# ReLU and row sum of a 64 MB tensor: another assignment of rows to partitions in the first 8 MB

## The chip, the cores and the metric

The kernel runs on one core of one Trainium2 chip. The metric is device time in microseconds, the median of several runs; less is better. Nothing else runs on the chip meanwhile.

## The reference

```python
def setup_inputs():
    batch, seq, dim = 32, 512, 1024
    return {"x": np.random.randn(batch, seq, dim).astype(np.float32)}

def reference(x):
    relu_x = np.maximum(x, 0)
    return np.sum(relu_x, axis=-1).astype(np.float32)
```

Negative values are set to zero and each row of 1024 floats is summed. The input has 32 x 512 = 16384 rows of 4 KB, 64 MB (67.11 million bytes) in all; the output is 16384 floats, 64 KB. Every input byte is read once.

## The kernel before

**Layout.** The rows, flattened to 16384 x 1024, are dealt to the 128 partitions of SBUF, 128 rows to each. This is done in two parts. The first `N1 = 128 * 16` rows, 8 MB, are viewed as `xf`: partition p holds rows 16p to 16p+15, one stretch of 64 KB in memory, and the stretches of neighbouring partitions are neighbours in memory. The other 14336 rows, 56 MB, are viewed as `xv`: partition p holds 112 rows one after the other, 448 KB, and a load takes 16 of the 112. So a load of 16 rows per partition always takes 128 contiguous runs of 64 KB; in the first load the runs lie 64 KB apart from one partition to the next, in the others 448 KB. The views `of` and `ov` of the output match `xf` and `xv`; the helpers `rows` and `sums` choose between them.

**Buffers and loads.** There are three buffers `io0` to `io2`, each 128 partitions x 16 rows x 1024 floats (8 MB). Seven loads of 8 MB (`NB = 7`) go round these three. Load j from j = 3 on waits until VectorE has finished with load j-3. The last 8 MB are loaded in smaller parts: 8 rows, 4 rows, and then a few pieces of the last 4 rows (`TAIL`, `START_PIECE`, `END_PIECE`, `PIECES`), so that little work is left when the last byte has landed.

**Who issues.** All loads and stores are issued by SyncE, through one queue (`load`, line 99; `store`, lines 109 and 110). There is no scheduler: the program is written out by hand, with one semaphore for each load, one that counts ScalarE's instructions and one that counts VectorE's. `open_without_barrier` moves the first load to the very start of the program, ahead of the branch into its body (`EARLY = 1`).

**Compute.** For the first five loads and most of the sixth, ScalarE (ACT) clamps the tile in place with a Relu activation (`clamp`, line 117), in one instruction or in two halves, and VectorE (DVE) sums each row with a reduction (`total`, line 125). The last rows are done row by row, with an instruction that clamps and sums at once, on ScalarE (`act_row`, line 132) or on VectorE (`dve_row`, line 140). The results collect in `res`, 128 x 128 floats.

**Stores.** Three at the end: the 16 columns of `res` that belong to the first load, 110 columns of the others, and the last 2.

Of the kernel before, what the change touches and what calls it, by code (L numbers as in the profile page):

```python
# [7 lines left out]
P = 128  # L8

ROWS = 16  # L10
NBUF = 3
# [8 lines left out]
TAIL = [8, 4]  # L20
START_PIECE, END_PIECE = 280, 260
PIECES = [240, 244]

EARLY = 1


def kernel(tc: tile.TileContext, x: bass.AP, out: bass.AP):
    nc = tc.nc
    sems = Semaphores(tc)

    tc.close()
    tc.compile()
    nc.cur_bb = nc.bb_map[tc.start_bb_name]
    body = nc.cur_bb.bb.instructions
    ends = list(body)
    body.clear()
    n_stores = relu_sum(nc, sems, x, out)
    body.extend(ends)


    nc.cur_bb = nc.bb_map[tc.start_bb_name + "_end"]
    nc.cur_bb.bb.instructions.clear()
    nums = sorted(s.num for s in (*sems.loads, sems.act, sems.dve))
    cleared = range(nums[0], nums[-1] + 1)
    assert len(cleared) == len(nums)
    nc.sync.sem_clear(cleared)
    nc.sync.wait_ge(sems.stored, 16 * n_stores).then_inc(sems.stored, -16 * n_stores)
    open_without_barrier(tc, EARLY)


class Semaphores:
    def __init__(self, tc: tile.TileContext):
        n = len(TWO) + len(TAIL) + 2 + len(PIECES)
        self.loads = [tc.alloc_semaphore(f"load{i}") for i in range(n)]
        self.act = tc.alloc_semaphore("act")
        self.dve = tc.alloc_semaphore("dve")
        self.stored = tc.alloc_semaphore("stored")


def relu_sum(nc, sems: Semaphores, x: bass.AP, out: bass.AP):  # L60
    x_flat = x.flatten_outer_dims()
# [3 lines left out]
    assert N == P * NT == P * ROWS * (NB + 1)  # L65
    assert sum(TAIL) == ROWS - 4 and START_PIECE + END_PIECE + sum(PIECES) == D

    bufs = [nc.alloc_sbuf_tensor(f"io{i}", [P, ROWS, D], F32) for i in range(NBUF)]
    res = nc.alloc_sbuf_tensor("res", [P, NT], F32)

    extra = len(PIECES) + 1
    parts = [
        nc.alloc_sbuf_tensor(f"piece{i}", [P, w + extra * (i + 1 == len(PIECES))], F32)
        for i, w in enumerate(PIECES)
    ]


    N1 = P * ROWS
    xf = x_flat[:N1].rearrange("(p m) d -> p m d", p=P)
    xv = x_flat[N1:].rearrange("(p m) d -> p m d", p=P)  # L80
    o_flat = out.rearrange("b s -> (b s)")
    of = o_flat[:N1].rearrange("(p m) -> p m", p=P)
    ov = o_flat[N1:].rearrange("(p m) -> p m", p=P)

    def rows(m, n):
        if m < ROWS:
            return xf[:, m : m + n, :]
        return xv[:, m - ROWS : m - ROWS + n, :]

    def sums(m, n):  # L90
        if m < ROWS:
            return of[:, m : m + n], res[:, m : m + n]
        return ov[:, m - ROWS : m - ROWS + n], res[:, m : m + n]

    n_load = n_act = n_dve = n_store = 0
# [1 line left out]
    def load(dst, src, after=None):  # L97
        nonlocal n_load
        dma = nc.sync.dma_start(out=dst, in_=src)  # L99
        if after:  # L100
            dma.wait_op(sems.dve, after[1], "sem-ge")
        dma.then_inc(sems.loads[n_load], 16)
        n_load += 1
        return sems.loads[n_load - 1]

    def store(m, n, act, dve):
        nonlocal n_store
        dst, src = sums(m, n)
        nc.sync.wait_ge(sems.act, act)
        nc.sync.dma_start(out=dst, in_=src).wait_op(sems.dve, dve, "sem-ge").then_inc(  # L110
            sems.stored, 16
        )
        n_store += 1

    def clamp(ap, loaded):
        nonlocal n_act
        i = nc.scalar.activation(out=ap, in_=ap, func=RELU)  # L117
        if loaded is not None:
            i.wait_op(loaded, 16, "sem-ge")
        i.then_inc(sems.act, 1)  # L120
        n_act += 1

    def total(ap, m, n):
        nonlocal n_dve
        nc.vector.tensor_reduce(  # L125
            out=res[:, m : m + n], in_=ap, axis=mybir.AxisListType.X, op=ADD
        ).wait_op(sems.act, n_act, "sem-ge").then_inc(sems.dve, 1)
        n_dve += 1

    def act_row(ap, accum_out, loaded):  # L130
        nonlocal n_act
        i = nc.scalar.activation(out=ap, in_=ap, func=RELU, accum_out=accum_out)  # L132
        if loaded is not None:
            i.wait_op(loaded, 16, "sem-ge")
        i.then_inc(sems.act, 1)
        n_act += 1

    def dve_row(ap, accum_out, loaded):
        nonlocal n_dve
        i = nc.vector.tensor_scalar(  # L140
            out=ap,
            in0=ap,
            scalar1=0.0,
            scalar2=None,
            op0=MAX,
            op1=ADD,
            accum_out=accum_out,
        )
        if loaded is not None:
            i.wait_op(loaded, 16, "sem-ge")  # L150
        i.then_inc(sems.dve, 1)
        n_dve += 1

    freed = []
    m = 0
    for j in range(NB):
        buf = bufs[j % NBUF]
        loaded = load(buf[:, :, :], rows(m, ROWS), j >= NBUF and freed[j - NBUF])
        c = 0
        act_waits = dve_waits = loaded  # L160
        for n in TWO[j]:
            clamp(buf[:, c : c + n, :], act_waits)
            total(buf[:, c : c + n, :], m + c, n)
            act_waits = None
            c += n
        for _ in range(ACT[j]):
            act_row(buf[:, c, :], res[:, m + c : m + c + 1], act_waits)
            act_waits = None
            c += 1
        for _ in range(DVE[j]):  # L170
            dve_row(buf[:, c, :], res[:, m + c : m + c + 1], dve_waits)
            dve_waits = None
            c += 1
        assert c == ROWS
        freed.append((n_act, n_dve))
        m += ROWS


    buf = bufs[NB % NBUF]
    c = 0  # L180
    for n in TAIL:
        loaded = load(
            buf[:, c : c + n, :], rows(m, n), None if c else freed[NB - NBUF]
        )
        for i in range(n):
            if i % 2 == 0 or (n == 8 and i == 7):
                act_row(buf[:, c, :], res[:, m : m + 1], loaded if i == 0 else None)
            else:
                dve_row(buf[:, c, :], res[:, m : m + 1], loaded if i == 1 else None)
            c += 1  # L190
            m += 1

    flat = buf[:, :, :].rearrange("p c d -> p (c d)")
    src = rows(m, 4).rearrange("p c d -> p (c d)")
    at = c * D
    split = 2 * D
    b = split + START_PIECE
    end = split + D - END_PIECE
    last, w = parts[-1], PIECES[-1]
    others = [last[:, w + i : w + i + 1] for i in range(extra)]  # L200
    loaded = load(flat[:, at : at + b], src[:, :b])
# [5 lines left out]
    loaded = load(flat[:, at + end : at + 4 * D], src[:, end:])  # L207
# [77 lines left out]
```

## Time and profile before

| what | value |
|---|---|
| median of 3 runs | 161.07 us (161.0 to 161.1) |
| the profiled execution, its own time | 160.96 us |
| its span | 159.6 us |
| VectorE busy | 117.6 us, 74% of the span |
| ScalarE busy | 104.2 us, 65% |
| DMA packets, share of 16 engines' span | 98.0% |
| HBM read | 67.11 MB, 421 GB/s over the span |
| ScalarE starts on loads 0, 1, 2 at | 21.87, 41.19, 60.55 us |

The span runs from the first instruction that the profile records to the last; the execution's own time lies 1.4 us above it. "Busy" counts an engine's own instructions, without those that issue transfers. The DMA figures are for the 16 DMA engines of the core, which carry all loads and stores. A DMA packet here is one contiguous run, 64 KB in the 8 MB loads. In a table by stretches of time a packet and its bytes are counted where the packet starts, so a short stretch can show more than the engines can move, and the next one less.

### The profile page before, as it was taken

Reading aid. Unit: us, or ns where it says so; the run is one execution under the profiler, and the core shown is the slowest. Engines: PE = TensorE matmul, PEld = TensorE weight load, DVE = VectorE, ACT = ScalarE, POOL = GpSimd, SP = SyncE. Lnnn points to the kernel's source line nnn. Section 1 sums busy time; section 2 is a strip of 40 time slices with the busy share of each in tenths; the row PEclk is TensorE's granted clock in tenths of the full one; section 3 lists DMA queues with packets and bytes.
Section 4 is the critical chain, followed back from the end, with each engine's and each line's share of the span. In section 5 each row is a group of like instructions: output and inputs, shape, how many; then the busy total and the mean of one; then the engine's idle time right before and its main releaser. Section 6 shows DMA issues by size and latency. Waiting matters only on the chain.

```text
span 159.6 us, 120 instructions
## 1 busy us (share of the span) xinstructions
DVE 117.6 (74%) x43; ACT 104.2 (65%) x50; POOL 0.2 (0%) x4
## 2 busy tenths in 40 slices
DVE  0000000009999499994999999999999999999986
ACT  3000059990699708996099951999329993499995
POOL 0000000000000000000000000000000000000000
DMA  7996996996997999979979969969969969798993
GB/s 279 509 526 263 526 526 263 526 509 279 526 476 312 526 394 394 526 345 443 526 328 460 526 263 526 526 263 526 509 279 526 493 296 526 337 452 382 418 412 119
DMA packets 2304, 67.18 MB, mean 421 GB/s; under 512 B 640, under 2 KB 896, under 8 KB 1024
## 3 DMA queue, kind: packets, MB, share of 16 engines
q1 hardware_dynamic: 2304, 67.18, 98.0%
HBM read 67.11 MB, written 0.07 MB: 421 GB/s over the span
## 4 chain that ended last, share of the span: by engine, by line
DMA 43%; DVE 34%; ACT 17%; another core or an unknown queue 3%; SPq 1%; issue 0%
DMA io<-in_x_dram 43%; DVE res L125 32%; ACT io L117 17%; DVE io L140 1%; SPq L99 1%; DVE piece L224 0%; DVE piece L140 0%
## 5 line engine op out<-in xcount | busy, mean ns | idle before, releaser
L125 DVE TENSOR_REDUCE res<-io 128x8 f32<-128x8192 f32 (+2 forms) x9 | 101.1, 11287 | 40.0 <-ACT io L117 40.0
L117 ACT ACTIVATE io<-io 128x8192 f32<-128x8192 f32 (+2 forms) x9 | 81.7, 9110 | 47.7 <-DMA io<-in_x_dram 47.7
L132 ACT ACTIVATE io<-io 128x1024 f32<-128x1024 f32 x20 | 20.9, 1045 | 6.0 <-DMA io<-in_x_dram 6.0
L140 DVE TENSOR_SCALAR_CACHE_REDUCE io<-io 128x1024 f32<-128x1024 f32 (+2 forms) x15 | 15.8, 1110 | 0.5 <-DMA io<-in_x_dram 0.4
L132 ACT ACTIVATION_READ_ACCUMULATOR io<-io 128x1 f32 x20 | 3.8, 188 | 0.0
L117 ACT ACT_TABLE_LOAD x1 | 1.3, 1283 | 0.1
L140 DVE DVE_READ_ACCUMULATOR io<-io 128x1 f32 x15 | 1.2, 82 | 0.0
L224 DVE TENSOR_SCALAR_CACHE_REDUCE piece<-piece 128x247 f32<-128x247 f32 x1 | 0.4, 410 | 0.0
L140 DVE TENSOR_SCALAR_CACHE_REDUCE piece<-piece 128x240 f32<-128x240 f32 x1 | 0.4, 397 | 0.0
L269 POOL MEMSET const-bfloat16-1.0<- 128x1 bf16 x1 | 0.1, 101 | 0.0
L269 POOL MEMSET const-uint8-127<- 128x1 uint8 x1 | 0.1, 101 | 0.0
L269 POOL MEMSET const-float32-0.0<- 128x1 f32 x1 | 0.1, 98 | 0.2 <-issue 0.2
L269 POOL MEMSET const-float32-1.0<- 128x1 f32 x1 | 0.1, 98 | 0.0
L224 DVE DVE_READ_ACCUMULATOR piece<-piece 128x1 f32 x1 | 0.1, 83 | 0.0
L140 DVE DVE_READ_ACCUMULATOR piece<-piece 128x1 f32 x1 | 0.1, 82 | 0.0
## 6 DMA issues: line engine op xcount, KB each, us to landing
io<-in_x_dram SPq DMA_DIRECT2D x1, 4096.0 KB, 21.6
io<-in_x_dram SPq DMA_DIRECT2D x1, 2048.0 KB, 26.1
io<-in_x_dram SPq DMA_DIRECT2D x1, 1164.0 KB, 28.4
io<-in_x_dram SPq DMA_DIRECT2D x1, 642.0 KB, 29.5
piece<-in_x_dram SPq DMA_DIRECT2D x1, 122.0 KB, 29.2
piece<-in_x_dram SPq DMA_DIRECT2D x1, 120.0 KB, 29.4
io<-in_x_dram SPq DMA_DIRECT2D x7, 26.9
out_dram<-res SPq DMA_DIRECT2D x1, 55.0 KB, 1.6
```

The source lines that it names most:

```text
L99: dma = nc.sync.dma_start(out=dst, in_=src)
L117: i = nc.scalar.activation(out=ap, in_=ap, func=RELU)
L125: nc.vector.tensor_reduce(out=res[:, m : m + n], in_=ap, axis=mybir.AxisListType.X, op=ADD).wait_op(sems.act, n_act, "sem-ge").then_inc(se ...
L132: i = nc.scalar.activation(out=ap, in_=ap, func=RELU, accum_out=accum_out)
L140: i = nc.vector.tensor_scalar(out=ap, in0=ap, scalar1=0.0, scalar2=None, op0=MAX, op1=ADD, accum_out=accum_out,)
L224: nc.vector.tensor_scalar(out=last[:, :], in0=last[:, :], scalar1=0.0, scalar2=None, op0=MAX, op1=ADD, accum_out=res[:, NT - 2 : NT - 1],) ...
L269: nc = _bacc.Bacc("TRN2", target_bir_lowering=False, num_devices=1)
```

## The change

The first 8 MB are cut into 128 stretches of 16 rows, 64 KB each, as before, but they go to other partitions. With `GROUP = 8`, stretch 16j+i (i from 0 to 15, j from 0 to 7) is put into partition 8i+j; before, stretch p was put into partition p. The source of the first load becomes a pattern of three dimensions, 16 (i, 64 KB apart) x 8 (j, 1 MB apart) x 16384 floats, and its destination is the whole buffer as 128 x 16384 floats. The store of the first 16 columns of sums goes through the matching view of the output, so that each sum lands where the reference has it. All other loads and stores, all compute instructions and all waits stay as they are.

```diff
+GROUP = 8
...
     N1 = P * ROWS
-    xf = x_flat[:N1].rearrange("(p m) d -> p m d", p=P)
+    xf = x_flat[:N1].rearrange("(j i m) d -> i j (m d)", j=GROUP, m=ROWS)
     xv = x_flat[N1:].rearrange("(p m) d -> p m d", p=P)
     o_flat = out.rearrange("b s -> (b s)")
-    of = o_flat[:N1].rearrange("(p m) -> p m", p=P)
+    of = o_flat[:N1].rearrange("(j i m) -> i j m", j=GROUP, m=ROWS)
     ov = o_flat[N1:].rearrange("(p m) -> p m", p=P)
 
     def rows(m, n):
-        if m < ROWS:
-            return xf[:, m : m + n, :]
         return xv[:, m - ROWS : m - ROWS + n, :]
 
     def sums(m, n):
         if m < ROWS:
-            return of[:, m : m + n], res[:, m : m + n]
+            return of, res[:, :ROWS]
         return ov[:, m - ROWS : m - ROWS + n], res[:, m : m + n]
...
     for j in range(NB):
         buf = bufs[j % NBUF]
-        loaded = load(buf[:, :, :], rows(m, ROWS), j >= NBUF and freed[j - NBUF])
+        if j == 0:
+            loaded = load(buf[:, :, :].rearrange("p m d -> p (m d)"), xf)
+        else:
+            loaded = load(buf[:, :, :], rows(m, ROWS), j >= NBUF and freed[j - NBUF])
```

## The prediction

> **What bounds the kernel now.** I read the page first, then the busy time by stage, then the chain of waits, then the first microseconds. The page's head and its queue part:
>
> ```profile
> span 159.6 us, 120 instructions
> DVE 117.6 (74%) x43; ACT 104.2 (65%) x50; POOL 0.2 (0%) x4
> ...
> q1 hardware_dynamic: 2304, 67.18, 98.0%
> HBM read 67.11 MB, written 0.07 MB: 421 GB/s over the span
> ```
>
> The reader is to see that no compute engine is near full, while the 16 DMA engines carry packets for 98.0% of the span. Next the busy time in stretches that I cut where the first three loads land (columns: DVE, ACT, POOL, PE clock, DMA share, GB/s):
>
> ```profile
> 0.00:21.85 21.85, 0.00 (x0) 1.28 (x1) 0.20 (x4) 1.00 1.02 432
> 21.85:41.20 19.35, 5.44 (x1) 13.87 (x2) 0.00 (x0) 1.00 1.00 434
> 41.20:60.53 19.33, 17.23 (x2) 13.85 (x1) 0.00 (x0) 1.00 1.00 434
> ```
>
> An 8 MB load takes 19.33 to 19.35 us at 434 GB/s, that is 27.1 GB/s for each of 16 engines, and the DMA share is 1.00. The waits say the same from the consumer's side:
>
> ```profile
> ACT io L117 <- DMA io<-in_x_dram: 47.7, 6, 20.5
> DVE res L125 <- ACT io L117: 40.0, 3, 35.8
> ```
>
> ACT waits for data, DVE for ACT; nothing waits for a free engine. So a microsecond added to or taken from the transfers of the first load moves every later load, and the end, by the same. One slack could absorb it: load 3 needs the buffer of load 0. It was issued at 53.00 us (the timeline, line L99), when loads 1 and 2 still had work until 60.53. But DVE frees that buffer a fixed 13.86 + 17.22 us after load 0 lands, and loads 1 and 2 move with load 0, so the slack of 7.5 us moves along and absorbs nothing.
>
> Last, the first round of packets:
>
> ```profile
> 0.00:1.00 1.00, 0.00 (x0) 0.88 (x1) 0.20 (x4) 1.00 0.00 0
> 1.00:1.40 0.40, 0.00 (x0) 0.40 (x1) 0.00 (x0) 1.00 6.25 2130
> 1.40:1.90 0.50, 0.00 (x0) 0.00 (x1) 0.00 (x0) 1.00 1.02 393
> 1.90:3.90 2.00, 0.00 (x0) 0.00 (x0) 0.00 (x0) 1.00 0.00 0
> 3.90:6.30 2.40, 0.00 (x0) 0.00 (x0) 0.00 (x0) 1.00 1.01 437
> ```
>
> A packet is booked where it starts. 2130 GB/s x 0.40 us is 0.85 MB, so 13 of the 16 first packets of 64 KB start between 1.0 and 1.4 us, the other three by 1.9. Their mean length is (6.25 x 0.40 + 1.02 x 0.50) = 3.01 us, against 19.34 / 8 = 2.42 us for a later one. The first round thus costs 0.59 us more than a later round. That is all that a better place to begin can give back.
>
> [...]
>
> **The change part by part.**
>
> *Compute, later loads, the other stores: nothing.* ACT and DVE see the same 128x16384 tile; their rows are the same in number and shape. The 8 KB store of the first sums goes to 16x8x16 places instead of 128x16, still 64 B each. It took 28.8 us to land behind the last loads; SP has only the two later stores behind it, and the next waits for data until about 155 us. Without that cover it would cost one SP issue, 0.34 us.
>
> *The first load's issue.* The source becomes 16 x 8 x 16384, a pattern with one more dimension. SP's issues at L99 took 327 to 457 ns; the first, at 383 ns, stands ahead of everything. A longer pattern was not seen: at best no change, at worst one more issue, 0.4 us. I take +0.2.
>
> *Where the engines begin in memory.* The 0.59 us of the first round could vanish wholly or not at all (or double). I take -0.3.
>
> *Where the engines write.* This is the large term. [...] each of the 8 packets takes 2 x 2.42 us: 8 x 2.42 = 19.34 us more. [...] with starts mostly within 0.4 us I take L = 0.2, so -0.4. [...]
>
> *Sum:* 19.34 - 0.4 + 0.2 - 0.3 = +18.8 us. The profiled execution has a span of 159.6 and a time of 160.96, 1.4 us around the span; it becomes 179.8. It stands 0.1 us under the median of 161.07, so 179.9 on the median, which I round to 180.0. What is late next is everything: load 0 lands near 40.7 instead of 21.87 us, and loads 1 to 6 keep their spacing.
>
> **Rivals.**
>
> [...] Then only the start counts: 161.07 - 0.59 + 0.2 = 160.7, at best 160.5. [...]
>
> *The pairs fall out of step.* [...] +9.7, about 170.8. The fixed length of packets in the trace (1.00 share in each stage) gives no hint of an order between engines. Partial favour lies between this and the main case, a later drift a little under it: 166 to 176.
>
> *The change doesn't do what it says.* [...] the time is that of before give or take the issue: 161.0 to 161.4.
>
> **How the numbers follow.** Fair sharing 0.65 (177 to 185), out of step 0.17 (166 to 176), [...] nothing changed 0.03, a bare loss at the issue 0.03 (161.4 to 163). From no change a measurement of this kernel can tell about 0.2%, 0.3 us. Slower: 0.65 + 0.17 + 0.03 = 0.85; faster 0.12; same 0.03. The range takes the first two cases, 166 to 185; it leaves out 0.18.
>
> **What would show each step.** In the profile after, the stretch from 0 to the landing of load 0 should run at about 218 GB/s with a DMA share near 1, because packets last 4.8 us instead of 2.42; the first ACT row should start at 40 to 41 us; later loads should land 19.3 us apart as now. Packets of 2.42 us in two groups, with ACT starting near 31.5, would be the out-of-step case. [...] if the mean first packet falls from 3.01 towards 2.42, the near start works. A load 0 far beyond 43 us would mean that reading 64 KB apart costs something by itself, which I do not price.

## The result, and the profile after

The changed kernel takes 182.38 us (median of 4 runs, 182.26 to 182.46) against 161.06 us for the kernel before: a ratio of 1.1324, 95% interval 1.1304 to 1.1343. It is 21.3 us slower, all of it in the first load. The head and the queue part of its page:

```profile
span 181.0 us, 120 instructions
DVE 117.6 (65%) x43; ACT 104.2 (58%) x50; POOL 0.2 (0%) x4
...
q1 hardware_dynamic: 2304, 67.18, 98.0%
...
HBM read 67.11 MB, written 0.07 MB: 371 GB/s over the span
```

The compute engines are busy for the same microseconds as before. The DMA engines move the same bytes in the same number of packets and are still "busy" for 98.0% of the span, yet the rate fell from 421 to 371 GB/s. A busy DMA engine is thus not a DMA engine at full speed: a packet of the first load lasts about 5.1 us instead of 2.42, as the lines below show, and all of it counts as busy. What makes it last is the question of the experiments. The busy time by stage, cut where loads 0, 1 and 2 land (columns: DVE, ACT, POOL, PE clock, DMA share, GB/s):

```profile
0.00:43.20 43.20, 0.00 (x0) 1.28 (x1) 0.20 (x4) 1.00 1.00 218
43.20:62.50 19.30, 5.37 (x1) 13.86 (x1) 0.00 (x0) 1.00 1.00 435
62.50:81.85 19.35, 17.30 (x2) 13.86 (x1) 0.00 (x0) 1.00 1.00 434
```

The DMA share is 1.00 in all three, the rate is half in the first alone. The 218 GB/s of the first line flatter it, as packets are booked where they start: 218 GB/s x 43.20 us is 9.4 MB, so the first packets of load 1 are in it. Loads 1 and 2 follow at 19.3 us as before. The start of that first load, closer:

```profile
1.00:1.40 0.40, 0.00 (x0) 0.40 (x1) 0.00 (x0) 1.00 0.00 0
1.40:2.30 0.90, 0.00 (x0) 0.00 (x0) 0.00 (x0) 1.00 5.24 1165
2.30:5.80 3.50, 0.00 (x0) 0.00 (x0) 0.00 (x0) 1.00 0.00 0
5.80:41.40 35.60, 0.00 (x0) 0.00 (x0) 0.00 (x0) 1.00 1.00 206
```

No packet starts before 1.4 us, where 13 of 16 had. The 16 first packets (1165 GB/s x 0.90 us is 1.05 MB) last 5.24 x 0.90 = 4.72 us on average instead of 3.01; the DMA share, like the bytes, is booked where a packet starts. The other seven rounds fill 35.6 us, 5.09 us each instead of 2.42. The waits and the timeline agree:

```profile
ACT io L118 <- DMA io<-in_x_dram: 69.1, 6, 41.8
...
43.24 13.86 ACT L118 ACTIVATE io<-io 128x16384 f32<-128x16384 f32 x1 [41.84 <-DMA io<-in_x_dram]
...
74.38 0.33 SPq L100 DMA_DIRECT2D io<-in_x_dram  x1
```

ACT starts on load 0 at 43.24 us instead of 21.87, 21.37 us later; load 3 is issued at 74.38 instead of 53.00 us, later by the same; the span ends 21.4 us later. Nothing downstream absorbed any of it.

### The profile page after: what moved, and what is told of

Its sections match the earlier page's. It is cut to its first block, busy times and chain, and to the rows that moved or that the text cites. A ratio compares the mean times of both kernels' runs of the same rounds, so it can differ in the third digit from the quotient of the medians.

```text
span 181.0 us, 120 instructions
## 1 busy us (share of the span) xinstructions
DVE 117.6 (65%) x43; ACT 104.2 (58%) x50; POOL 0.2 (0%) x4
## 4 chain that ended last, share of the span: by engine, by line
DMA 40%; DVE 30%; ACT 23%; another core or an unknown queue 6%; SPq 0%; issue 0%
DMA io<-in_x_dram 40%; DVE res L126 29%; ACT io L118 23%; DVE io L141 1%; SPq L100 0%; DVE piece L228 0%; DVE piece L141 0%
```

## The experiments

Three theories could explain a halved first load: P, engines that write into certain partitions at the same time hold each other up; S, the order in which the engines read memory; F, the three-dimensional pattern itself. The prediction takes it that P doubles the length of every packet, and its 19.34 us rest on that. This was my assumption: nothing in the trace before shows it, and no trace names the engine that writes a partition. They show rates, lengths of packets and the share of engines at work, and it is by these that P is tested. Each kernel below is the kernel before with an altered first load, except the second.

**e1, two plain loads of 64 partitions.**

```diff
-        loaded = load(buf[:, :, :], rows(m, ROWS), j >= NBUF and freed[j - NBUF])
+        if j == 0:
+            w = P // PARTS                 # PARTS = 2
+            for q in range(PARTS):
+                dma = nc.sync.dma_start(
+                    out=buf[q * w : q * w + w, :, :],
+                    in_=xf[q * w : q * w + w, :, :],
+                )
+                dma.then_inc(sems.loads[0], 16)
...
```

> The kernel before, with its first 8 MB loaded as two plain loads of 64 partitions each, partition p still holding stretch p. Theory P [...]: [...] Load 0 lands near 43 us, its stretch runs at 205 to 210 GB/s, the time is 181.5 to 182.5 us. Theory S (the order in which the engines read memory): order as before, about 161 us. Theory F (the three-dimensional pattern is what is slow): plain pattern, about 161 us.

Measured: 182.35 us, one run; ACT starts on load 0 at 43.31 us. Its stretch of seven rounds:

```profile
5.70:41.30 35.60, 0.00 (x0) 0.00 (x0) 0.00 (x0) 1.00 1.00 206
```

The same 206 GB/s as the changed kernel, from a plain pattern, with each stretch of memory in the partition of before. S and F fall as causes of the halving.

**e2, the changed kernel with another source order.**

```diff
-    xf = x_flat[:N1].rearrange("(j i m) d -> i j (m d)", j=GROUP, m=ROWS)
+    S = ROWS * D
+    xf = bass.AP(x_flat.tensor, 0, [[9 * S, ROWS], [S, GROUP], [1, S]])
```

> The changed kernel with only the source of the first load altered: partition 8i+j gets stretch 9i+j[...]; the sums of the first 2048 rows are therefore of other rows. Theory P: destination as in the changed kernel, so no difference, load 0 lands at 43.2 us and the time is 182.4 within 0.5. Theory S: the near, interleaved order is gone, so 161 to 162 us. Theory F: the pattern keeps its three dimensions, 182.4 us.

Measured: 183.05 us, one run; load 0 lands at 44.14 us.

```profile
5.90:41.50 35.60, 0.00 (x0) 0.00 (x0) 0.00 (x0) 1.00 1.00 206
```

Again 206 GB/s. The source order has no part in the halving. The total is 0.7 us over the changed kernel, 0.2 more than I had allowed; landing is 0.9 us later. With one run the cause of that stays open, and a small part of the source order in it isn't ruled out.

**e3 and e4, a near start with the partitions outermost.** In both, neighbouring partitions begin 16 KB apart in memory instead of 64 KB. e3 lets them read overlapping memory; e4 deals the rows out anew inside the first 8 MB (its destination and its store of the sums are viewed to match).

```diff
-    xf = x_flat[:N1].rearrange("(p m) d -> p m d", p=P)
+    xf = bass.AP(x_flat.tensor, 0, [[4 * D, P], [D, ROWS], [1, D]])          # e3
+    xf = x_flat[:N1].rearrange("(n p r) d -> p n (r d)", p=P, r=NEAR)        # e4, NEAR = 4
```

> The kernel before, with the first load's partitions starting 16 KB apart in memory instead of 64 KB, each still reading 64 KB: neighbours overlap, and the sums of the first 2048 rows are of other rows. [...] Theory P: no slowdown, packets of 2.42 us, load 0 lands at 21.3 to 21.9 us; if a near start shortens the first packets (3.01 us in the kernel before), 160.5 to 160.9 us, if it does nothing 161.1. Theory S: near streams slow each other, well over 165 us. Theory F: 161.1 us.

> The kernel before, with the first 8 MB cut into runs of 4 rows (16 KB): partition p holds run p of each of four 2 MB regions. The output is the reference's. The first load is a three-dimensional pattern, 128 x 4 x 4096, [...] but the partition dimension is outermost on both sides[...]. Theory P: load 0 at about 434 GB/s, landing near 22 us, time 160.7 to 161.6 us (0.3 us for the longer issue, up to -0.6 for a near start). Theory F: a load of this form takes twice as long, about 180 us. Theory S: slower, in between.

Measured: e3 161.47 us, ratio 1.0024 (1.0016 to 1.0032). e4 161.68 us, ratio 1.0032 (1.0019 to 1.0045), and its first load, up to its landing:

```profile
0.00:21.90 21.90, 0.00 (x0) 1.28 (x1) 0.20 (x4) 1.00 1.02 431
```

So a three-dimensional pattern that keeps the partitions outermost on both sides runs at 431 GB/s (432 in the same stretch of the kernel before), and partitions that begin 16 KB apart cost no more than the 0.2 to 0.3% of these ratios: P holds, F and S fall again. Neither kernel gained from the near start. In e4 the first load isn't what is slower: in its profiled run, which took 162.15 us, ACT starts on load 0 at 21.93 us against 21.87, and on load 5 still only 0.09 us late. The rest came after that, in the smaller loads and stores at the end; its cause stays open. In e3 the first packets, which begin at these times, grew to 6.93 x 0.40 + 0.42 x 1.30 = 3.32 us from 3.01:

```profile
1.00:1.40 0.40, 0.00 (x0) 0.40 (x1) 0.00 (x0) 1.00 6.93 2130
1.40:2.70 1.30, 0.00 (x0) 0.00 (x1) 0.00 (x0) 1.00 0.42 151
```

e3 missed all three values given for it by 0.3 us or more; part of it may be that its neighbours read the same rows, which I did not separate.

**e5, eight plain loads of 16 partitions**: the kernel of e1 with `PARTS = 8`.

> The kernel before, with its first 8 MB loaded as eight plain loads of 16 partitions each, partition p still holding stretch p. [...] Theory P: each 64 KB packet takes four times 2.42 us, 9.7 us, or 10.2 to 10.4 if sharing costs the same 5 per cent that packets of 5.11 us showed over 4.84; load 0 runs at 102 to 109 GB/s and lands at 78 to 85 us, the time is 217 to 225 us. A rival Q, that anything but the plain split over 128 partitions runs at a fixed half rate, says 182 us.

Measured: 216.32 us, one run; load 0 lands at 77.21 us. Six of its rounds:

```profile
10.50:66.50 56.00, 0.00 (x0) 0.00 (x0) 0.00 (x0) 1.00 1.00 112
```

A packet takes 56.0 / 6 = 9.33 us. Loads of 16 partitions run at 112 GB/s where loads of 64 ran at 206, so the fixed half rate of rival Q falls. That a packet would take four times as long was an assumption; it took 9.33 / 2.42 = 3.9 times. 112 GB/s is above the 102 to 109 that I expected: the landing and the total came out just under the stated ranges. Why, this run does not show. My guess is that an engine ahead of the others was at times writing the next 16 partitions already.

**e6, the issue alone.**

```diff
+        nc.dge_precook = j > 0
         loaded = load(buf[:, :, :], rows(m, ROWS), j >= NBUF and freed[j - NBUF])
```

> The kernel before, with the switch dge_precook off for the first load alone: its pattern stays 128 x 16384[...]. It should show what of the change is the issue itself: the first issue at 0.6 to 0.7 us instead of 0.38, the first packets at 1.3 to 1.5 instead of 1.0 us, the time 161.2 to 161.5 us. If the later start of the changed kernel (1.45 us) comes from the three dimensions instead, 161.0 us.

Measured: 161.33 us, ratio 1.0017 (1.0009 to 1.0026). The SP queue's own timeline of this kernel, and then the first packets:

```profile
0.00 0.55 SPq L99 DMA_DIRECT2D io<-in_x_dram  x1
```

```profile
1.00:1.30 0.30, 0.00 (x0) 0.30 (x1) 0.00 (x0) 1.00 0.00 0
1.30:1.90 0.60, 0.00 (x0) 0.10 (x1) 0.00 (x0) 1.00 5.34 1748
```

The issue takes 0.55 us, less than the 0.6 to 0.7 that I expected: it lies between the 0.38 of before and the changed kernel's 0.68. The first packets start after 1.3 us, and the time is in the stated range. So 0.27 us on the median come with the longer issue. The rest of the changed kernel's delay (no packet before 1.4 us) isn't due to a third dimension as such: e4 has one too, its issue takes 0.44 us, and 15 of its 16 first packets start between 1.0 and 1.4 us (614 GB/s x 0.40 us is 0.25 MB, and its packets have 16 KB):

```profile
0.00 0.44 SPq L101
1.00:1.40 0.40, 0.00 (x0) 0.40 (x1) 0.00 (x0) 1.00 2.33 614
```

**e7, a far start**: e3 with `128 * D` for `4 * D`.

> The kernel before, with the first load's partitions starting 512 KB apart in memory instead of 64 KB [...]; the sums of the first 2048 rows are of other rows. If the distance between the places where the engines begin matters at all, as the change supposes, the mean first packet should be clearly longer than 3.01 us and the time 161.3 to 162.5 us; if it does not matter, 161.0 within 0.2. Theory P: [...] no large loss in either case.

Measured: 161.50 us, ratio 1.0039 (1.0027 to 1.0051); load 0 lands at 22.34 us, as it does in e3 (22.32).

```profile
1.00:1.40 0.40, 0.00 (x0) 0.40 (x1) 0.00 (x0) 1.00 2.46 819
1.40:2.60 1.20, 0.00 (x0) 0.00 (x1) 0.00 (x0) 1.00 1.55 601
```

The expectation was half right. The time rose as it said, but not because first packets were longer: their mean is 2.46 x 0.40 + 1.55 x 1.20 = 2.84 us. They start later, only 5 of 16 before 1.4 us (819 x 0.40 is 0.33 MB). The 16 KB between partitions in e3 and the 512 KB here both come out some 0.4 us slower than the 64 KB of before; against 21 us that is nothing.

**e8 and e9, eight partitions at a time, four apart or two apart.** In the slowed kernels so far an engine may also write into other partitions than it does in the kernel before, and rival A says that this is what makes it slow. e8 and e9 differ only in the eight partitions of a load, and the stretches that belong to them.

```diff
+            for at in (*range(64, 68), *range(96, 100), *range(4), *range(32, 36)):   # e8
+            for at in [16 * (q ^ 4) + r for q in range(8) for r in range(2)]:         # e9
+                dma = nc.sync.dma_start(
+                    out=buf[at : at + 29 : 4, :, :],       # e8; in e9 at : at + 15 : 2
+                    in_=xf[at : at + 29 : 4, :, :],
+                )
+                dma.then_inc(sems.loads[0], 16)
...
+            nc.sync.wait_ge(loaded, 16 * PARTS)            # PARTS = 16
```

> The kernel before, with its first 8 MB loaded by 16 loads of 8 partitions that lie four apart (64, 68 to 92 first, then 65, 69 and so on; the partitions from 0 last). A load of 8 partitions runs on 8 engines, one partition each[...]. SP waits for all of load 0 before it issues load 1, so that nothing else is on the way. Theory P (only sharing costs): packets of 2.42 us throughout, 8 engines at 217 GB/s, load 0 lands at 39.5 to 41.5 us, the time 181 to 184 us with the wait. Rival A [...]: the first eight loads take 5.1 us a packet, the last eight 2.42, load 0 lands near 62 us, the time is over 200 us.

> The same 16 loads on 8 engines, but the 8 partitions of a load lie two apart (64, 66 to 78 and so on)[...]. Theory P: packets of about 5.1 us as in the changed kernel, load 0 lands at 79 to 84 us, the time 221 to 227 us. [...] If packets of 5.1 us in the changed kernel (and not 4.84) come from all 16 engines being at work and not from the pairing, packets here take 4.7 to 4.85 us and load 0 lands at 77 to 79 us.

Measured: e8 183.43 us and e9 223.29 us, one run each; load 0 lands at 41.63 and 81.71 us. First e8, in its first eight loads (partitions 64 to 127) and its last eight (0 to 63); then e9, in its steady stretch and in two single loads, the second and the third:

```profile
6.85:18.95 12.10, 0.00 (x0) 0.00 (x0) 0.00 (x0) 1.00 0.50 217
21.40:38.45 17.05, 0.00 (x0) 0.00 (x0) 0.00 (x0) 1.00 0.50 215
```

```profile
10.80:74.72 63.92, 0.00 (x0) 0.00 (x0) 0.00 (x0) 1.00 0.50 107
5.70:10.80 5.10, 0.00 (x0) 0.00 (x0) 0.00 (x0) 1.00 0.50 103
10.80:15.60 4.80, 0.00 (x0) 0.00 (x0) 0.00 (x0) 1.00 0.50 109
```

Half of the 16 engines are at work in both (share 0.50). With the partitions four apart, each of the 8 moves 27 GB/s (217 / 8 and 215 / 8) in the upper 64 partitions and in the lower, so rival A falls: it had the first eight loads at half the rate of the last eight, and the landing near 62 us. With the partitions two apart, each moves 107 / 8 = 13.4 GB/s. With the same number of loads, engines and bytes, and the same wait, partitions two apart instead of four double the time up to the landing, 81.71 us against 41.63. P is shown in this form: which partitions are written at the same time decides the rate. What eight partitions two apart share and eight four apart do not, no trace shows. The last possibility in the expectation of e9, that the 5.1 us come from 16 engines being at work, falls too: both totals lie in the ranges of P, and the packets of e9's second load last 0.50 x 5.10 x 16 / 8 = 5.1 us with 8 engines. Those of its third last 4.8 us; the last section comes back to that.

## Why the prediction was right, and where its sizes were off

**The bound and the chain: right.** The first load's delay went through to the end without loss, 21.37 us at its landing and 21.4 us in the span. The slack in front of load 3 moved along, as worked out.

**The mechanism: right as far as the runs show it.** The destination decides: e1 runs at 206 GB/s with a plain pattern, e2 at 206 with another source order, and e8 and e9 at 217 and 107 with other sets of partitions. The half rate that I had assumed came out a little lower, 206 GB/s against 434; which engines hold each other up, and through what, is not shown. The engines stayed in step: seven rounds of 5.09 us fill 35.6 us without a faster group, so the out-of-step rival, the rival in which only the start counts, and the one in which nothing changes are all out. One sign came true by accident: the stretch up to the landing reads 218 GB/s as foretold, but only because packets of load 1 are booked in it.

**The sum: 18.8 expected, 21.4 measured.** The mis-sized terms, in the order of their weight:

- *Two times 2.42 us a packet.* Seven rounds took 5.09 instead of 4.84 us: 7 x 0.25 = 1.8 us more. Each of the 16 engines moved 206 / 16 = 12.9 GB/s on average, not the half of 27.1.
- *The lead of one engine over another, -0.4.* This was an estimate of what one gains by starting ahead, L being the lead. One of the seven rounds is some 0.1 us shorter than the others (the last section has the lines), which is in the 5.09 already; that a lead makes it shorter is not shown. A lead at the very start would be in the first round.
- *The landing, not in the sum.* In the changed kernel the first packets of load 1 have all started by 42.35 us, so load 0's last packets were through; ACT starts 0.9 us after. In the kernel before, they have all started by 21.55 us, 0.3 us ahead of the landing. The packet records in the traces agree: from the end of load 0's last packet to ACT's start it is 0.90 us in the changed kernel and 0.38 in the one before, 0.5 more. The delay is longer where packets are longer: 0.37 us in e8 (packets of 2.42 us), 0.83 in e1 (5.09) and 0.89 in e9 (4.8 to 5.1), 1.39 in e5 (9.33). What happens in that time no run shows.
- *The issue, +0.2.* The first packets start about 0.4 us later; e6 shows 0.27 of it in the time.
- *The first round, 4.84 + 0.59 - 0.3 = 5.13 us.* It took 4.72, 0.4 us less. The slow start may hide in part behind the longer packets, or the lead of an engine may be in it; no run tells these apart.

1.8 + 0.4 + 0.5 + 0.2 - 0.4 = 2.5 of the 2.6 us.

**The hoped-for gain at the start: absent.** I took -0.3 of a possible -0.59. e4, whose partitions begin 16 KB apart and whose first load ran at 431 GB/s, has its first load landed 0.06 us after the kernel before, with an issue 0.06 us longer. No run here shows a gain from a nearer start.

## What to carry to other kernels

Look at both access patterns of a load, not only at how contiguous the source is. Here a source with 16 outermost, against 128 partitions at the destination, took twice as long as the plain load (206 GB/s against 434), and so did plain loads over 64 partitions each (e1, 206). A DMA share of 1.00 doesn't show it; the GB/s beside it and the duration of a packet do. In e4, which reorders the rows but leaves the partitions outermost on both sides, the first load kept its full rate, 431 GB/s.

## What the runs showed of the hardware that I had not expected

A packet of the changed kernel's first load takes more than twice the 2.42 us of a plain load, and in one round less than in the others. The packets of three rounds of the changed kernel, the second, the fifth and the seventh:

```profile
5.80:6.80 1.00, 0.00 (x0) 0.00 (x0) 0.00 (x0) 1.00 5.11 1049
21.10:22.10 1.00, 0.00 (x0) 0.00 (x0) 0.00 (x0) 1.00 4.99 1049
31.20:32.20 1.00, 0.00 (x0) 0.00 (x0) 0.00 (x0) 1.00 5.11 1049
```

Each line holds 16 packets (1049 GB/s x 1.00 us is 1.05 MB), so 5.11 x 1.00 us is their mean length: 65.5 KB in 5.11 us, 12.8 GB/s for an engine, where half of the 27.1 of a plain load (434 / 16) would be 13.6. Those of the fifth round take 4.99 us. In e9 the second load fills the odd partitions between the even ones of the first, 64 to 79, and takes 5.1 us a packet; the third goes to the next sixteen partitions and takes 4.8. So 5.1 us were measured with 16 engines at work and with 8.

My guess for the shorter packets is the lead that the prediction reckoned with: an engine that is ahead goes over to other partitions first and leaves the old ones to the engines behind it. No run varied the lead or shows which partitions an engine writes. Why a packet takes more than twice 2.42 us, and what sets the 27.1 GB/s of an engine, stays open.
